# The first block of a decoder trunk: how a conditioning vector, x and two of its rows reach the engines

## The chip, the cores and the metric

The kernel runs on one core of a Trainium2 chip. The core has five engines with a queue of instructions each: TensorE (PE: matrix products and transposes), VectorE (DVE), ScalarE (ACT), GpSimd (POOL) and SyncE (SP, which here only issues DMA transfers). The metric is the device time of one execution in microseconds (us), the median of several.

## The reference

One layer of a hybrid decoder over x (2048 tokens by 1024 channels), float32. A condition vector c (1024) gives 6 x 1024 numbers that shift, scale and gate the two sub-layers:

```python
c_act = jax.nn.silu(c)
mod = (c_act @ w_ada[l] + b_ada[l])[:, None, :]
sh1, sc1, g1, sh2, sc2, g2 = jnp.split(mod, 6, axis=-1)
h = rms_norm(x) * (1.0 + sc1) + sh1
x = x + g1 * token_mixer(h, w_in[l], ...)
h = rms_norm(x) * (1.0 + sc2) + sh2
x = x + g2 * conv_ffn(h, w_up[l], ...)
return rms_norm(x) * final_gain
```

Only the start matters here: the first 512 tokens of `x`, the first two parts of `mod` (sh1 and sc1), `h` for those tokens, and the first products `h @ w_in`.

## The kernel before, in words

Channels lie on the 128 partitions, so x is 8 tiles (k = 0 to 7) of 128 channels, and tokens are taken in blocks of 512. `mod` is kept as 48 columns of 128 numbers: columns 0 to 7 are sh1, 8 to 15 are sc1. A column m needs the 128 x 1024 tile `wada[m]` (512 KB). `ada(m)`, called as `cond(m)` in the first block, is one DVE instruction (line 199): it multiplies that tile by `c_act`, in which the whole of silu(c) stands on every partition, and adds up along the row into `mod[:, m]`; a second, tiny DVE row reads the sum out. `c_act` comes from `craw`, a DMA that copies c to all 128 partitions (line 178).

Products are made at nearly float32 precision from rounded parts: a weight tile is cast on ACT to a high part (`hf`, `hq`, `hv0`, `hv1`, line 408, later `hhfh`, `hhqh`, `hvgh`, line 242), and DVE subtracts to get the low part (`lf`, `lq`, `lv`, line 412). Likewise h for channel tile k is made in three steps: `scaled` (DVE, line 365, x times scale times `bc`, the spread 1/rms), `high` (ACT, line 369, adds the shift and rounds) and `low` (DVE, line 372). Each k then feeds 18 products of TensorE ("the products of k", lines 453 and 459): two with `hf`, two with `hq`, eight with `hv`, one with `lf`, one with `lq`, four with `lv`. The first product of k needs `high`, the second needs `low`.

`startup()` writes out this first block by hand, and the order in which it calls things is the order of the DVE, ACT and SP queues there; TensorE's order is also the written one everywhere. Behind the first block the tile framework orders DVE, ACT and SP by priorities. Before the loop over k come the squares of x (`sumsq`: ACT squares, line 358, DVE adds, line 359), four products that sum them over channels (`ssn`), Newton steps for 1/sqrt on DVE, and `bcn`, which spreads the result (copied to `bc` by ACT, line 442). The loop over k is driven by the table `plan`.

What follows the first block starts with the next head's products `pshfh` (line 254). The four accumulators of TensorE are all in use by the first block, so the first of these products must wait until ACT has read the accumulator of `hf` twice (`sfh` and `snh`, two sigmoids, lines 742 and 743); ACT also makes that head's weight parts. Weight tiles are loaded into two buffers (`NRAW = 2`), so the load of `rv0` (third weight tile) waits until `lf` has been made from the first. `masks` (224 KB) and `alraw` (64 KB) are two small inputs that are needed later; both take a buffer of the pool `te`, and so do all tiles made by `tmp()`. Low parts are also written back to DRAM for reuse (`keep`, tiles `kepti0l`, `kepti1l` and so on).

Of the kernel before, what the change touches and what calls it, by code (L numbers as in the profile page):

```python
# [18 lines left out]
P = 128  # L19
# [85 lines left out]
def trunk(ctx, tc, xT, vecs, cvec, cst, rope, msk, wada, win, walow, wgla, wout, wup, wdown, out):  # L105
# [33 lines left out]
    def small(name, n=8):  # L139
        return pc.tile([P, n], F32, tag="sm", name=name, bufs=8)  # L140

    V, S, G, T = nc.vector, nc.scalar, nc.gpsimd, nc.tensor

    vec = pc.tile([P, NV], F32, tag="vec", name="vec")
    nc.sync.dma_start(vec[:], vecs)
    c_all = pc.tile([P, NC_], F32, tag="cst", name="c_all")
    m_all = p1.tile([P, NM], U32, tag="msk", name="m_all")
    ident = c_all[:, C_ID:C_ID + P]
    causal = c_all[:, C_CAUS:C_CAUS + P]
    ones = c_all[:, C_ONE:C_ONE + 1]  # L150
    nc.sync.dma_start(c_all[:], cst)

    def newton(x, y, n):

# [19 lines left out]


    c_act = pa.tile([P, D], F32, tag="a4k", name="c_act")
    craw = pa.tile([P, D], F32, tag="a4k", name="craw")
    nc.sync.dma_start(craw[:], cvec.to_broadcast([P, D]))
    S.activation(c_act[:], craw[:], AF.Sigmoid)
    V.tensor_tensor(c_act[:], c_act[:], craw[:], op=ALU.mult)  # L180
    mod = pc.tile([P, 48], F32, tag="mod", name="mod")

    bada1 = vec[:, V_BADA:V_BADA + 48]
# [180 lines left out]
    def scaled(t, bc, k):  # L364
        V.scalar_tensor_tensor(t, t, SC1[:, k:k + 1], bc, op0=ALU.mult, op1=ALU.mult)

    def high(t, k, name):
        h[k] = ph.tile([P, 2, TB], F32R, tag="h", name=f"ha{name}{k}", bufs=8)
        S.activation(h[k][:, 0, :], t, AF.Identity, bias=SH1[:, k:k + 1])

    def low(t, k):
        V.scalar_tensor_tensor(h[k][:, 1, :], t, SH1[:, k:k + 1], h[k][:, 0, :], op0=ALU.add, op1=ALU.subtract)
# [5 lines left out]
    def x_tile(name, k):  # L378

        if k % 2 == 0:  # L380
            pair[0] = px.tile([P, SB], F32, tag="xy", name=name, bufs=4)
        return pair[0][:, (k % 2) * TB:(k % 2 + 1) * TB]
# [6 lines left out]
    def startup():  # L389


        x, W, pending = [], {}, []
        for k in range(KD):
            x.append(x_tile(f"x0_{k}", k))
            nc.sync.dma_start(x[k], xT[0, :, k, :])
        raws = {}

        def weight(name, i, extra=False):
            raw = pw.tile([P, 1024], F32, tag="wraw", name="r" + name, bufs=NRAW)
            nc.sync.dma_start(raw[:], win[i])  # L400
            if extra:
                t = [pa.tile([P, 1024], F32R, tag="a4k", name=n + name) for n in "hl"]
            else:
                t = [pw.tile([P, 1024], F32R, tag="w" + n, name=n[0] + name) for n in ("hi", "lo")]
            W[name] = [*t, raw, i]

        def cast(name):
            S.copy(W[name][0][:], W[name][2][:])

        def low_part(name):  # L410
            hi, lo, raw, i = W[name]
            V.tensor_tensor(lo[:], raw[:], hi[:], op=ALU.subtract)

        def cond(m):
            ada(m, raws.pop(m))

        def load(*ms):
            for m in ms:
                raws[m] = ada_load(m, True)
        load(8, 0)  # L420
        weight("f", 1)
        load(9)
        weight("q", 0)
        load(1, 2)
        acc = new_acc("n1_0")
        for k in range(KD):
            sumsq(acc, x[k], k, "n1_0_")
        cond(8)
        ps = late_ps("ssn1_0")
        for c in range(NCH):  # L430
            T.matmul(ps[:, c:c + 1], acc[:, c * P:(c + 1) * P], ones, start=True, stop=True)
        ms, r = small("msn1_0", NCH), small("rsn1_0", NCH)
        V.tensor_scalar(ms[:], ps[:, 0:NCH], 1.0 / D, EPS, op0=ALU.mult, op1=ALU.add)
        newton(ms, r, NCH)
        cast("f")
        bc = bc1[0] = new_bc1(0)
        ps = late_ps("bcn1_0")
        for c in range(NCH):
            T.transpose(ps[:, c * P:(c + 1) * P], r[:, c:c + 1].to_broadcast([P, P]), ident)
        cond(0)  # L440
        cond(9)
        S.copy(bc[:], ps[:])
        cast("q")
        pf, pq = acc_ps("pshfh0_0"), acc_ps("pshqh0_0")
        pv = [acc_ps(f"psvgh0_0_{j}") for j in range(NCH // 2)]

        def put(kind, k, w):

            two = (0, 1) if w == 0 else (0,)
            if kind in "fq":  # L450
                sl = slice(k * P, (k + 1) * P)
                for p in two:
                    T.matmul((pf if kind == "f" else pq)[:], W[kind][w][:, sl], h[k][:, p, :],
                             start=k == 0 and w == 0 and p == 0, stop=k == KD - 1 and w == 1, skip_group_check=True)
            else:
                sl = slice((k % 4) * 256, (k % 4 + 1) * 256)
                for c in range(NCH):
                    for p in two:
                        T.matmul(pv[c // 2][:, (c % 2) * 256:(c % 2) * 256 + 256], h[k][:, p, c * P:(c + 1) * P],
                                 W[f"v{k // 4}"][w][:, sl], start=k == 0 and w == 0 and p == 0 and c % 2 == 0,  # L460
                                 stop=k == KD - 1 and w == 1 and c % 2 == 1, skip_group_check=True)

        def flush():
            for q in list(pending):
                if (q[0] if q[0] in "fq" else f"v{q[1] // 4}") in parts[q[2]]:
                    pending.remove(q)
                    put(*q)

        plan = [((10,), (), (1,), "f"), ((3, 11), (), (2,), "q"), ((4,), (10,), (3,), "v0"),
                ((12, 5), (11,), (4,), None), ((13, 6), (12,), (5,), "v1"), ((14, 7), (13,), (6,), None),  # L470
                ((15,), (14,), (7,), None), ((), (15,), (), None)]
        parts = {"f", "q"}, set()
        for k, (ld, first, then, wl) in enumerate(plan):
            if k == 0:
                weight("v0", 2)
            if k == 3:
                weight("v1", 3, True)
            load(*ld)
            for m in first:
                cond(m)  # L480
            scaled(x[k], bc[:], k)
            high(x[k], k, "0_")
            if k in (1, 4):
                name = "v0" if k == 1 else "v1"
                cast(name)
                parts[0].add(name)
            for m in then:
                cond(m)
            low(x[k], k)
            if wl:  # L490
                low_part(wl)
                parts[1].add(wl)
            pending += [(kind, k, w) for w in (0, 1) for kind in "fqv"]
            flush()
        assert not pending
        ready["hfh0_0"], ready["hqh0_0"], ready["vgh0_0"] = pf, pq, pv
        return W

# [1162 lines left out]
```

## Time and profile before

| what | us |
|---|---|
| median of 3 runs (lowest, highest) | 2534.34 (2533.82, 2537.03) |
| the profiled execution | 2533.74 |
| its span, from first to last instruction | 2532.0 |
| TensorE busy (97% of the span) | 2454.5 |
| VectorE busy (79%) | 1988.6 |
| ScalarE busy (46%) | 1153.5 |
| first product of line 453 | 22.82 |
| first product behind the first block (line 254) | 58.88 |

The profile is one execution; its time is 1.7 us over its span. Start times below are counted from the first instruction. A busy share of 97% for TensorE says that nearly all time behind the first block is TensorE's own work, which the change leaves in the same order.

### The profile page before, as it was taken

The numbers are of one execution on the slowest core, as the hardware profiler recorded it, in microseconds if no ns is written. First come the engines' busy times: TensorE is split into PE (matmuls) and PEld (weight loads), VectorE is DVE, ScalarE is ACT, GpSimd is POOL, SyncE is SP. The second block draws the span as 40 slices with busy tenths as digits, with TensorE's granted clock in tenths as the row PEclk, the third lists the DMA queues.
The fourth block names the chain that finished last, engine by engine and source line by source line (L and its number), as shares of the span: only waits on it lengthen the run. The fifth ranks groups of instructions, "written<-read, shape, count | busy, mean of one in ns | idle before, by whom it ended". The sixth has DMA issues, their size and how long they took to land.

```text
span 2532.0 us, 35188 instructions
## 1 busy us (share of the span) xinstructions
PE 2454.5 (97%) x12173; PEld 2064.3 (82%) x12173; DVE 1988.6 (79%) x3642; ACT 1153.5 (46%) x1960; POOL 150.0 (6%) x278
## 2 busy tenths in 40 slices
PE   5999999999999999999899999999989999999998
PEld 4888878888888888788788888888878888888887
DVE  8987887877688685877798888887688777778666
ACT  3333424434443334434455455555445555555453
POOL 1000000000000000000110000000001010010000
PEclk9999999999999999999999999999999999999999
DMA  8854459865688647884654544587665544447763
GB/s 309 296 163 134 169 181 320 289 225 169 218 284 310 223 159 242 308 303 161 215 187 149 168 154 138 168 283 242 209 219 170 160 138 150 152 136 256 218 191 133
DMA packets 232498, 525.11 MB, mean 207 GB/s; under 512 B 24928, under 2 KB 28032, under 8 KB 232320
## 3 DMA queue, kind: packets, MB, share of 16 engines
q1 hardware_dynamic: 229120, 512.38, 61.2%
q0 software_dynamic: 3200, 10.49, 1.2%
q8 instruction: 96, 1.57, 0.2%
q14 instruction: 82, 0.67, 0.1%
HBM read 397.46 MB, written 125.30 MB: 206 GB/s over the span
## 4 chain that ended last, share of the span: by engine, by line
PE 46%; DMA 2%; DVE 1%; issue 1%; ACT 0%; DVEq 0%; POOL 0%; SPq 0%; ACTq 0%; POOLq 0%
PE X L254 6%; PE X L255 6%; PE X L256 6%; PE Z L254 3%; PE Z L255 3%; PE Z L256 3%; PE dX L254 3%; PE dX L256 3%; PE dX L255 3%; PE dY L254 2%; PE dY L256 2%; PE dY L255 2%; PE Y L254 2%; PE Y L255 2%; PE Y L256 2%
## 5 line engine op out<-in xcount | busy, mean ns | idle before, releaser
L254 PE MATMUL X<-B,A 128*128 128x512 f32 x572 | 224.5, 392 | 1.8 <-ACT u L1355 1.8
L256 PE MATMUL X<-B,A 128*128 128x512 f32 x572 | 223.8, 391 | 0.0
L255 PE MATMUL X<-B,A 128*128 128x512 f32 x572 | 223.8, 391 | 0.0
L1055 DVE TENSOR_TENSOR dA<-rd,dA 128x512 fp32r<-128x512 f32 x154 | 105.9, 689 | 85.9 <-ACT dA L1054 85.7
L1054 ACT CAST dA<-rd 128x512 fp32r<-128x512 f32 x154 | 95.6, 621 | 134.3 <-PE dY L256 44.7
L1055 DVE TENSOR_TENSOR A<-s,A 128x512 fp32r<-128x512 f32 x176 | 120.5, 685 | 39.0 <-ACT A L1054 38.6
L1054 ACT CAST A<-s 128x512 fp32r<-128x512 f32 x176 | 108.7, 618 | 69.1 <-PE Z L256 44.9
L254 PE MATMUL dX<-dB,dA 128*128 128x512 f32 x352 | 136.9, 389 | 0.0
L255 PE MATMUL dX<-dB,dA 128*128 128x512 f32 x352 | 136.9, 389 | 0.0
L256 PE MATMUL dX<-dB,dA 128*128 128x512 f32 x352 | 136.9, 389 | 0.0
L254 PEld LDWEIGHTS X<-B,A 128*128 128x128 f32 x572 | 108.2, 189 | 25.4 <-ACT u L1355 3.1
L256 PEld LDWEIGHTS X<-B,A 128*128 128x128 f32 x572 | 108.1, 189 | 22.8
L255 PEld LDWEIGHTS X<-B,A 128*128 128x128 f32 x572 | 108.1, 189 | 22.3
L254 PE MATMUL Z<-B,A 128*128 128x512 f32 x308 | 119.9, 389 | 0.0
L255 PE MATMUL Z<-B,A 128*128 128x512 f32 x308 | 119.8, 389 | 0.0
L256 PE MATMUL Z<-B,A 128*128 128x512 f32 x308 | 119.8, 389 | 0.0
L1055 DVE TENSOR_TENSOR dB<-rb,dB 128x512 fp32r<-128x512 f32 x154 | 105.4, 685 | 11.5 <-ACT dB L1054 11.5
L1055 DVE TENSOR_TENSOR A<-r,A 128x512 fp32r<-128x512 f32 x130 | 89.3, 687 | 29.5 <-ACT A L1054 29.3
L662 PEld LDWEIGHTS lvh<-qbh,kh 128*128 128x128 f32 x768 | 100.1, 191 | 14.4 <-issue 7.3
L1054 ACT CAST A<-r 128x512 fp32r<-128x512 f32 x130 | 80.8, 622 | 63.7 <-PE Z L256 59.2
L662 PE MATMUL lvh<-qbh,kh 128*128 128x128 f32 x768 | 102.1, 275 | 5.5 <-DVE kh L672 5.2
L254 PE MATMUL psqkvgr<-hqkvgr,ha 128*128 128x512 f32 x256 | 106.1, 414 | 1.1 <-DVE orsg L160 1.0
(479 smaller groups left out, 7000.2 us busy)
## 6 DMA issues: line engine op xcount, KB each, us to landing
gs<-yv SPq DMA_DIRECT2D x154, 256.0 KB, 3.0
rb<-gs SPq DMA_DIRECT2D x154, 256.0 KB, 4.1
r<-wup SPq DMA_DIRECT2D x140, 256.0 KB, 3.4
s<-sumsu SPq DMA_DIRECT2D x136, 256.0 KB, 3.2
wada<-wada SPq DMA_DIRECT2D x48, 512.0 KB, 6.6
rd<-sumsd SPq DMA_DIRECT2D x88, 256.0 KB, 3.8
rd<-wdown SPq DMA_DIRECT2D x66, 256.0 KB, 4.0
x<-xT SPq DMA_DIRECT2D x64, 256.0 KB, 5.9
```

Source lines behind the costliest of these rows:

```text
L254: T.matmul(ps, lhs[0], rhs[0], start=first, stop=False, skip_group_check=more)
L255: T.matmul(ps, lhs[0], rhs[1], start=False, stop=False, skip_group_check=more)
L256: T.matmul(ps, lhs[1], rhs[0], start=False, stop=last, skip_group_check=more)
L662: T.matmul(ps[:, c * P:(c + 1) * P].rearrange("p (h n s) -> p h n s", h=2, s=s), kq[:, c * P:(c + 1) * P], rhs, start=True, stop=True)
L1054: S.copy(hi, src)
L1055: V.tensor_tensor(lo, src, hi, op=ALU.subtract)
```

## The change

1. The condition vector is loaded as 8 rows of 128 numbers (`c8`), silu is taken on those, and TensorE spreads them over the partitions: eight products with a column of the identity matrix, repeated 128 times (`cc0`, `cc1`), copied to `c_act` half by DVE and half by ACT. A transposed copy `ccol` is made as well.
2. x comes in four transfers of 512 KB in place of eight of 256 KB, with the first tiles of `wada` between them; `masks` and `alraw` are issued later.
3. Columns 15 and 7 of `mod` are made by TensorE: `row_spread` transposes the tile `wada[m]` in eight pieces (`wt15`, `wt7`) that ACT copies out, `row_sum` makes one row of 128 sums with eight products (`wm15`, `wm7`), which ACT copies (`wr15`, `wr7`), and `row_end` turns the row into a column with one product (`we15`, `we7`), which ACT adds the bias to. `row_spread` stands behind k = 2 and 4, `row_sum` behind 3 and 5, `row_end` behind 4 and 6.
4. The other columns are made by DVE at other places; `cond(8)` and `cond(0)` come ahead of the Newton steps. A table `steps` sets the order for each k (s = scaled, c = cond, h = high, l = low).

```diff
@@ -141,14 +141,16 @@
 
     V, S, G, T = nc.vector, nc.scalar, nc.gpsimd, nc.tensor
 
+    c_all = pc.tile([P, NC_], F32, tag="cst", name="c_all")
+    nc.sync.dma_start(c_all[:], cst)
+    c8, c8s = (tmp(n)[:, 0:P] for n in ("c8", "c8s"))
+    nc.sync.dma_start(c8[0:KD, :], cvec.rearrange("o (k p) -> (o k) p", p=P))
     vec = pc.tile([P, NV], F32, tag="vec", name="vec")
     nc.sync.dma_start(vec[:], vecs)
-    c_all = pc.tile([P, NC_], F32, tag="cst", name="c_all")
     m_all = p1.tile([P, NM], U32, tag="msk", name="m_all")
     ident = c_all[:, C_ID:C_ID + P]
     causal = c_all[:, C_CAUS:C_CAUS + P]
     ones = c_all[:, C_ONE:C_ONE + 1]
-    nc.sync.dma_start(c_all[:], cst)
 
     def newton(x, y, n):
 
@@ -174,10 +176,9 @@
 
 
     c_act = pa.tile([P, D], F32, tag="a4k", name="c_act")
-    craw = pa.tile([P, D], F32, tag="a4k", name="craw")
-    nc.sync.dma_start(craw[:], cvec.to_broadcast([P, D]))
-    S.activation(c_act[:], craw[:], AF.Sigmoid)
-    V.tensor_tensor(c_act[:], c_act[:], craw[:], op=ALU.mult)
+    ccol = small("ccol", KD)
+    S.activation(c8s[0:KD, :], c8[0:KD, :], AF.Sigmoid)
+    V.tensor_tensor(c8s[0:KD, :], c8s[0:KD, :], c8[0:KD, :], op=ALU.mult)
     mod = pc.tile([P, 48], F32, tag="mod", name="mod")
 
     bada1 = vec[:, V_BADA:V_BADA + 48]
@@ -389,11 +390,11 @@
     def startup():
 
 
-        x, W, pending = [], {}, []
-        for k in range(KD):
-            x.append(x_tile(f"x0_{k}", k))
-            nc.sync.dma_start(x[k], xT[0, :, k, :])
-        raws = {}
+        x, W, pending, raws = [], {}, [], {}
+
+        def x_load(i):
+            x.extend((x_tile(f"x0_{2 * i}", 0), x_tile(f"x0_{2 * i + 1}", 1)))
+            nc.sync.dma_start(pair[0][:].rearrange("p (a n) -> p a n", a=2), xT[0, :, 2 * i:2 * i + 2, :])
 
         def weight(name, i, extra=False):
             raw = pw.tile([P, 1024], F32, tag="wraw", name="r" + name, bufs=NRAW)
@@ -417,30 +418,71 @@
         def load(*ms):
             for m in ms:
                 raws[m] = ada_load(m, True)
-        load(8, 0)
+
+        def row_spread(m):
+
+            raw, halves = raws.pop(m), []
+            for j in range(2):
+                p = lev_ps(f"wt{m}_{j}")
+                for i in range(4):
+                    T.transpose(p[:, i * P:(i + 1) * P], raw[:, (4 * j + i) * P:(4 * j + i + 1) * P], ident)
+                t = tmp(f"wt{m}_{j}")
+                S.copy(t[:], p[:])
+                halves.append(t)
+            return m, halves
+
+        def row_sum(m, halves):
+            p = late_ps(f"wm{m}")
+            for i in range(KD):
+                T.matmul(p[0:1, 0:P], ccol[:, i:i + 1], halves[i // 4][:, (i % 4) * P:(i % 4 + 1) * P],
+                         start=i == 0, stop=i == KD - 1)
+            row = tmp(f"wr{m}")
+            S.copy(row[0:1, 0:P], p[0:1, 0:P])
+            return m, row
+
+        def row_end(m, row):
+            p = late_ps(f"we{m}")
+            T.matmul(p[:, 0:1], row[0:1, 0:P], ones[0:1, :], start=True, stop=True)
+            S.activation(mod[:, m:m + 1], p[:, 0:1], AF.Identity, bias=bada1[:, m:m + 1])
+
+        x_load(0)
+        load(8)
+        x_load(1)
+        load(0)
+        x_load(2)
+        x_load(3)
+        load(9)
         weight("f", 1)
-        load(9)
+        load(1)
         weight("q", 0)
-        load(1, 2)
+        load(10, 2)
+        for j in range(2):
+            p = lev_ps(f"cc{j}")
+            for i in range(4 * j, 4 * j + 4):
+                T.matmul(p[:, (i % 4) * P:(i % 4 + 1) * P], ident[0:KD, i:i + 1].to_broadcast([KD, P]), c8s[0:KD, :],
+                         start=True, stop=True)
+            (S.copy if j else V.tensor_copy)(c_act[:, j * 512:(j + 1) * 512], p[:])
+        p = late_ps("ccol")
+        T.transpose(p[:, 0:KD], c8s[0:KD, :], ident[0:KD, 0:KD])
+        S.copy(ccol[:], p[:, 0:KD])
+        cond(8)
         acc = new_acc("n1_0")
         for k in range(KD):
             sumsq(acc, x[k], k, "n1_0_")
-        cond(8)
+        cond(0)
         ps = late_ps("ssn1_0")
         for c in range(NCH):
             T.matmul(ps[:, c:c + 1], acc[:, c * P:(c + 1) * P], ones, start=True, stop=True)
         ms, r = small("msn1_0", NCH), small("rsn1_0", NCH)
         V.tensor_scalar(ms[:], ps[:, 0:NCH], 1.0 / D, EPS, op0=ALU.mult, op1=ALU.add)
         newton(ms, r, NCH)
-        cast("f")
         bc = bc1[0] = new_bc1(0)
         ps = late_ps("bcn1_0")
         for c in range(NCH):
             T.transpose(ps[:, c * P:(c + 1) * P], r[:, c:c + 1].to_broadcast([P, P]), ident)
-        cond(0)
         cond(9)
+        cast("f")
         S.copy(bc[:], ps[:])
-        cast("q")
         pf, pq = acc_ps("pshfh0_0"), acc_ps("pshqh0_0")
         pv = [acc_ps(f"psvgh0_0_{j}") for j in range(NCH // 2)]
 
@@ -466,33 +508,43 @@
                     pending.remove(q)
                     put(*q)
 
-        plan = [((10,), (), (1,), "f"), ((3, 11), (), (2,), "q"), ((4,), (10,), (3,), "v0"),
-                ((12, 5), (11,), (4,), None), ((13, 6), (12,), (5,), "v1"), ((14, 7), (13,), (6,), None),
-                ((15,), (14,), (7,), None), ((), (15,), (), None)]
-        parts = {"f", "q"}, set()
-        for k, (ld, first, then, wl) in enumerate(plan):
+        loads = [(11,), (3, 15, 12), (4, 7), (13, 5, 14), (6,), (), (), ()]
+        casts = ["q", "v0", None, "v1", None, None, None, None]
+        steps = ["s0 c1 h lf l c10", "s1 h c2 lq l", "s2 h c11 lv0 l", "s3 c3 h c12 l", "s4 c4 h lv1 l c13",
+                 "s5 c5 h c14 l", "s6 c6 h s7 l", "h l"]
+        parts = {"f"}, set()
+        rows = []
+        for k in range(KD):
             if k == 0:
                 weight("v0", 2)
-            if k == 3:
+            if k == 2:
                 weight("v1", 3, True)
-            load(*ld)
-            for m in first:
-                cond(m)
-            scaled(x[k], bc[:], k)
-            high(x[k], k, "0_")
-            if k in (1, 4):
-                name = "v0" if k == 1 else "v1"
-                cast(name)
-                parts[0].add(name)
-            for m in then:
-                cond(m)
-            low(x[k], k)
-            if wl:
-                low_part(wl)
-                parts[1].add(wl)
+            load(*loads[k])
+            for st in steps[k].split():
+                kind, what = st[0], st[1:]
+                if kind == "s":
+                    scaled(x[int(what)], bc[:], int(what))
+                elif kind == "c":
+                    cond(int(what))
+                elif kind == "h":
+                    high(x[k], k, "0_")
+                    if casts[k]:
+                        cast(casts[k])
+                        parts[0].add(casts[k])
+                elif what:
+                    low_part(what)
+                    parts[1].add(what)
+                else:
+                    low(x[k], k)
             pending += [(kind, k, w) for w in (0, 1) for kind in "fqv"]
+            if k in (2, 4):
+                rows.append(row_spread({2: 15, 4: 7}[k]))
             flush()
-        assert not pending
+            if k in (3, 5):
+                rows.append(row_sum(*rows.pop()))
+            if k in (4, 6):
+                row_end(*rows.pop(0))
+        assert not pending and not rows
         ready["hfh0_0"], ready["hqh0_0"], ready["vgh0_0"] = pf, pq, pv
         return W
 
```

ScalarE's queue around k = 3 to 6, before (`ha0_k` is the high part of h for tile k, `hhfh` and `hhqh` belong to the next head):

```order
L369 ACTIVATE ha0_3_529<-x0_2_348,mod_104 128x512
L369 ACTIVATE ha0_4_557<-x0_4_351,mod_104 128x512
L408 CAST hv1_521<-rv1_519 128x1024
L242 CAST hhfh0_1_722<-rhfh0_1_724 128x1024
L369 ACTIVATE ha0_5_587<-x0_4_351,mod_104 128x512
L369 ACTIVATE ha0_6_613<-x0_6_354,mod_104 128x512
```

The same place in the changed kernel:

```order
L370 ACTIVATE ha0_3_564<-x0_2_351,mod_106 128x512
L409 CAST hv1_504<-rv1_502 128x1024
L440 COPY wr15_596<-wm15_587 1x128
L370 ACTIVATE ha0_4_602<-x0_4_355,mod_106 128x512
L430 COPY wt7_0_612<-wt7_0_607 128x512
L430 COPY wt7_1_619<-wt7_1_614 128x512
L446 ACTIVATE mod_106<-we15_639,vec_89 128x1
L243 CAST hhfh0_1_789<-rhfh0_1_791 128x1024
L370 ACTIVATE ha0_5_644<-x0_4_355,mod_106 128x512
L440 COPY wr7_675<-wm7_666 1x128
L370 ACTIVATE ha0_6_679<-x0_6_357,mod_106 128x512
```

Between the `high` steps stand copies that read what TensorE has just made: `wr15` ahead of `ha0_4`, the bias step of `we15` ahead of `ha0_5`, `wr7` ahead of `ha0_6`.

ScalarE's queue at the end of the first block, before:

```order
L369 ACTIVATE ha0_7_637<-x0_6_354,mod_104 128x512
L242 CAST hhqh0_1_763<-rhqh0_1_765 128x1024
L742 ACTIVATE sfh0_0_685<-pshfh0_0_429 128x512
L743 ACTIVATE snh0_0_686<-pshfh0_0_429 128x512
L748 ACTIVATE sqh0_0_691<-pshqh0_0_430 128x512
```

And in the changed kernel (`alow` is cast from the late input `alraw`, `hvgh` is a weight part of the next head, which stood eight rows further back):

```order
L829 CAST alow_123<-alraw_734 128x8x16
L446 ACTIVATE mod_106<-we7_701,vec_89 128x1
L370 ACTIVATE ha0_7_704<-x0_6_357,mod_106 128x512
L243 CAST hhqh0_1_830<-rhqh0_1_832 128x1024
L243 CAST hvgh0_1_0_905<-rvgh0_1_0_907 128x1024
L794 ACT_TABLE_LOAD
L794 ACTIVATE sfh0_0_752<-pshfh0_0_443 128x512
L795 ACTIVATE snh0_0_753<-pshfh0_0_443 128x512
```

A cast, a load of ScalarE's function table and, further up, the cast of `alow` now stand ahead of the two sigmoids.

TensorE's queue from the last products of k = 3 to the first of k = 4, before:

```order
L453 MATMUL pshqh0_0_430<-ha0_3_529,lq_370 128x512
L459 MATMUL psvgh0_0_0_431<-lv0_436,ha0_3_529 128x256 x2
L459 MATMUL psvgh0_0_1_432<-lv0_436,ha0_3_529 128x256 x2
L453 MATMUL pshfh0_0_429<-ha0_4_557,hf_363 128x512 x2
L453 MATMUL pshqh0_0_430<-ha0_4_557,hq_369 128x512 x2
```

In the changed kernel:

```order
L495 MATMUL pshqh0_0_444<-ha0_3_564,lq_370 128x512
L501 MATMUL psvgh0_0_0_445<-lv0_450,ha0_3_564 128x256 x2
L501 MATMUL psvgh0_0_1_446<-lv0_450,ha0_3_564 128x256 x2
L437 MATMUL wm15_587<-wt15_0_521,ccol_103 1x128 x4
L437 MATMUL wm15_587<-wt15_1_528,ccol_103 1x128 x4
L428 MATMUL wt7_0_607<-c_all_84,wada7_508 128x128 x4
L428 MATMUL wt7_1_614<-c_all_84,wada7_508 128x128 x4
L495 MATMUL pshfh0_0_443<-ha0_4_602,hf_363 128x512 x2
```

The sums `wm15` stand behind all products of k = 3, and the transposes `wt7` between them and k = 4. From the next head on TensorE's rows are the same in both kernels.

## Rows read from the trace of the kernel before

**Rows 1.** Stretches: us; busy us and count of each engine; TensorE clock, DMA share, GB/s.

```profile
45.00:50.00 5.00, 3.33 (x15) 2.54 (x14) 4.93 (x10) 0.84 (x2) 0.00 (x0) 0.83 0.94 373
...
140.00:150.00 10.00, 10.00 (x68) 8.95 (x66) 6.52 (x18) 4.92 (x10) 0.90 (x2) 1.00 0.85 276
```

**Rows 2.** TensorE in order of time: start, us, operation, [idle before <- releaser].

```profile
29.75 2.08 PE L459 MATMUL psvgh<-hv,ha 128*128 128x256 f32 x8 [3.74 <-ACT hv L408]
...
42.13 0.39 PE L453 MATMUL pshfh<-ha,hf 128*128 128x512 f32 x1
...
47.91 0.50 PE L453 MATMUL pshfh<-ha,hf 128*128 128x512 f32 x1 [0.62 <-DVE ha L372]
...
52.13 0.62 PE L453 MATMUL pshfh<-ha,hf 128*128 128x512 f32 x2
...
54.93 0.39 PE L453 MATMUL pshfh<-ha,hf 128*128 128x512 f32 x1
55.56 0.50 PE L453 MATMUL pshfh<-ha,hf 128*128 128x512 f32 x1 [0.23 <-DVE ha L372]
...
58.88 0.50 PE L254 MATMUL pshfh<-ha,hhfh 128*128 128x512 f32 x1 [0.48 <-ACT snh L743]
...
68.52 0.60 PE L639 MATMUL dth<-c_all,xh 128*128 128x128 f32 x4
...
73.66 1.07 PE L662 MATMUL lvh<-qbh,kh 128*128 128x128 f32 x8
74.48 0.37 PE L254 MATMUL psvgh<-hvgh,ha 128*128 128x256 f32 x1
...
177.62 0.50 PE L254 MATMUL psvgh<-hvgh,ha 128*128 128x512 f32 x1 [3.66 <-DVE sqh L749]
```

**Rows 3.** VectorE in order of time, from the sums to the last low part.

```profile
9.38 5.47 DVE L359 TENSOR_TENSOR san<-san,sqn 128x512 f32<-128x512 f32 x7 [0.77 <-ACT sqn L358]
...
16.80 0.16 DVE L433 TENSOR_SCALAR msn<-ssn 128x4 f32<-128x4 f32 x1 [0.76 <-PE ssn L431]
...
21.26 0.74 DVE L365 SCALAR_TENSOR_TENSOR x<-x,mod,bc 128x512 f32<-128x512 f32 x1
21.93 1.27 DVE L199 CUSTOM_DVE_ANT_0 wada<-wada,c_act,vec 128x1024 f32<-128x1024 f32 x1
...
23.13 0.74 DVE L372 SCALAR_TENSOR_TENSOR ha<-x,mod,ha 128x512 fp32r<-128x512 f32 x1
23.80 1.22 DVE L412 TENSOR_TENSOR lf<-rf,hf 128x1024 fp32r<-128x1024 f32 x1
...
54.76 0.74 DVE L372 SCALAR_TENSOR_TENSOR ha<-x,mod,ha 128x512 fp32r<-128x512 f32 x1
```

**Rows 4.** ScalarE in order of time, first block.

```profile
3.17 0.20 ACT L168 ACTIVATE lbe<-lbe 128x4 f32<-128x4 f32 x1 [1.15 <-DVE lbe L167]
3.39 1.28 ACT L179 ACT_TABLE_LOAD   x1
...
20.14 0.59 ACT L442 COPY bc<-bcn 128x512 f32<-128x512 f32 x1 [2.50 <-PE bcn L439]
...
28.65 1.04 ACT L408 CAST hv<-rv 128x1024 fp32r<-128x1024 f32 x1 [2.21 <-DMA rv<-win]
...
46.02 0.72 ACT L369 ACTIVATE ha<-x,mod 128x512 fp32r<-128x512 f32 x1 [2.38 <-DVE x L365]
...
56.09 1.05 ACT L242 CAST hhqh<-rhqh 128x1024 fp32r<-128x1024 f32 x1 [1.63 <-PE pshfh L453]
57.74 0.60 ACT L742 ACTIVATE sfh<-pshfh 128x512 f32<-128x512 f32 x1 [0.60 <-PE pshfh L453]
58.24 0.59 ACT L743 ACTIVATE snh<-pshfh 128x512 f32<-128x512 f32 x1
```

**Rows 5.** DMA issues of the first 60 us: count, KB, us from issue to landing.

```profile
kepti5l<-lhfh SPq DMA_DIRECT2D x1, 512.0 KB, 3.1
...
alraw<-walow SPq DMA_DIRECT2D x1, 64.0 KB, 8.4
```

## The prediction

> **What bounds the kernel now.** I read the table of stretches first. Late in the first block VectorE works 4.93 of 5 us while TensorE works 3.33 and its clock is partly lowered (0.83 over the stretch) [rows 1]; so there the chain of VectorE sets the pace. Then I followed the engines in order of time. Behind 58.88, where the next head's products begin, TensorE keeps its own order in both kernels, and a shift of that row shifts the end. The one long wait for VectorE further on, 3.66 us at 177.62, comes after a stretch (140 to 150) in which VectorE has 3.5 us to spare, so VectorE's earlier backlog is gone by then and the wait will come again, only later [rows 1, 2]. So the question is when the row at 58.88 starts. It waits for the second sigmoid, which ends at 58.83, which waits for the products of k = 7, which wait for the last low part at 54.76 to 55.50 [rows 2 to 4].
>
> **The front.** Spreading c takes eight products. Before has none so early; the nearest are the `lvh` products, four in 74.48 - 73.66 = 0.82 us, 0.205 each [rows 2]. The engine is cold here, so I take twice that, 3.3 us for eight. c8 is there at about 4 (VectorE's first row, which lets ScalarE's row at 3.17 go, waits for the same transfers [rows 4]); 4 + 3.3, a copy out of at most 0.59 and column 8 at 1.20 (21.93 to 23.13) give 9.1, while the adds now start at 9.38 [rows 3, 4]. They are seven in 5.47 us, held by ScalarE's squares as much as by x, so x in four transfers gains nothing here, and neither loses as long as the last pair lands by some 12.5. Column 0 fills the wait for `ssn` (which ends at 16.80) that column 8 fills now [rows 3]. One column fewer stands behind the Newton steps: the first `scaled` can start when `bc` is copied, 20.14 + 0.59 = 20.73, in place of 21.26: -0.5 us [rows 3, 4]. Bounds: 0 and +2, the latter if the spread is late by its whole 2 x 0.82.
>
> **What VectorE gains.** Columns 15 and 7 leave it (2.4 us) and column 0 is out of the chain. From 20.73 to `scaled` of k = 4 it has four `scaled` and four `low` at 0.67, six columns at 1.20 and three low weight parts at 1.22: 5.4 + 7.2 + 3.7 = 16.2, so x of k = 4 is ready at 36.9 + 0.75 = 37.7 [rows 3].
>
> **What TensorE and ScalarE get.** The load of `rv0` waits for `lf`. `lf` now stands ahead of `low` of k = 0, so it is 0.67 + 0.5 earlier, and the cast of `hv0` (28.65) and the first `hv` products (29.75) move to 28.6 [rows 2 to 4]. From there to the first product of k = 4 TensorE takes 42.13 - 29.75 = 12.38 us without a pause [rows 2]. It now also does the transposes `wt15` (two rows like the one of 0.60 for four, with run-out: 1.0 together) and the eight sums `wm15` at 0.205, 1.64 [rows 2]. That is 28.6 + 12.4 + 1.0 + 1.7 = 43.7. ScalarE's queue has `wr15`, which waits for these sums, ahead of `high` of k = 4. A small ScalarE row is 0.20 [rows 4]; with the notice 0.25. So `high` of k = 4 starts at 43.95, 6.2 us after its input is ready, and VectorE's gain is spent waiting.
>
> From then on the two engines hand over to each other, since each `high` stands behind a copy that needs the end of TensorE's work on the k before. One round: `high` 0.72, `low` 0.75 and two notices of 0.06 (46.02 + 0.72 = 46.74; 47.91 is the second product of k = 5), and 2.57 from the second product to the end of the 18: at the full clock k = 6 takes 54.93 - 52.13 = 2.80, less 0.23 for the first (0.62 for two, 0.39 for one) [rows 2 to 4]. That is 4.16.
> - k = 4: plus `we15` (0.2 and its run-out 0.1), the bias step 0.25, and the cast `hhfh`, which now stands ahead of `high`: 0.95 (a cast row is 1.05 and overlaps the next by 0.1) [rows 4]. 5.66; `high` of k = 5 at 49.6.
> - k = 5: plus `wm7` 1.64 + 0.15 and `wr7` 0.25: 6.2; k = 6 at 55.8.
> - k = 6: plus `we7` and the bias step: 4.7; k = 7 at 60.5.
> - k = 7: 1.59 to the second product; `hhqh` is free 0.53 later (55.56 to 56.09) and takes 1.0; behind it now stand `hvgh` 1.0, a table load 1.28 (before, the sigmoids found their table loaded) and the sigmoids 0.50 + 0.64 (57.74, 58.24, 58.88) [rows 2, 4]. 6.55; the next head starts at 67.05.
>
> That is 67.05 - 58.88 = +8.2 us. The waits of 1 to 2 us in each round are like those ahead of 47.91, behind which k = 5 ran at the lower clock: 52.13 - 47.91 = 4.22 in place of 2.57 [rows 1, 2]. I take one such round, +1.65; bounds none and four. Then 2533.74 + 9.85 = 2543.6 for an execution like the profiled one; the median of before lies 0.6 above that one, so **2544.2**.
>
> ScalarE's table load in the trace starts 0.02 us after the row ahead of it ends (3.37 to 3.39) and takes 1.28, which is what the sum has [rows 4]. The Trainium skill, "ScalarE: Activation LUTs", "What ACT_TABLE_LOAD costs", gives 1.28 for the load, as the row has it, but 2.66 for a switch with a drain. By that the time would be 1.4 higher; the row shows no drain ahead of it, and what follows it there waits for a transfer.
>
> Hidden: `masks` now come some 35 us later, but its readers on VectorE are the steps of the next head's `lvh`, the first of which is at 73.66; if they were later than that, TensorE would wait [rows 2]. The halves of `c_act` on ScalarE and the copies `wt15`, `wt7` (0.59 each) run while ScalarE has nothing else, or while TensorE works on the k before.
>
> **Rivals.**
> - *VectorE still sets the pace, faster.* If TensorE had `wm15` done by 37.7, the chain would be VectorE's: 37.7, then five columns, two weight parts and seven steps of 0.67 (6.0 + 2.4 + 4.7) end the last `low` at 50.8 rather than 55.50, and from there 0.06 + 0.53 + 1.0 + 1.0 + 1.28 + 1.14 = 5.0 rather than 3.38: start at 55.8, -3.1, 2531.2. For it speaks that VectorE was the bound [rows 1]; against it that TensorE would have to do in 9 us what the rows give 15 for. Chance 0.05.
> - *Within 0.2%* (5.1 us, about what a measurement tells from no change). If TensorE's first products ran at the full clock (three k at 2.80 and 1.7 of k = 0 are 10.1 in place of 12.4, -2.3), no round fell to the lower one (-1.65) and the four small copies cost 0.1 each less notice (-0.8): +5.1 or less. 0.08.
> - *`alraw` late.* `high` of k = 7 also stands behind the cast of `alow`, and `alraw` is issued behind `kepti5l`, which waits for `lhfh`. VectorE ends `low` of k = 5 at 51.1, then two `scaled`, column 6 and `lhfh` end at 54.9. A write like `kepti5l` lands in 3.1, with `masks` and `alraw` behind it some 0.8 more: 58.8, ahead of 60.5, no cost. In the crowded queue of before `alraw` took 8.4 [rows 5]: 63.3, +2.8 or 2547. 0.15.
> - *The clock falls in every round.* Three rounds more at 1.65: +4.95, 2549.2. For it: each round has the pattern of 45 to 48 [rows 1, 2]; against: k = 6 and 7 of before also had short waits and ran at full. 0.12. The Trainium skill, "TensorE: Matmul & The Clock Gate", "A second HAM failure mode: psum-queue depth-cycling", tells of a kernel whose short pauses between groups of matmuls make the clock swing between its two levels; by that rule this would be the outcome, and the trace has it in one round of eight so far.
>
> **How the numbers follow.** The forecast itself (0.60) has its own range of 2541.5 to 2547. The low end of the whole range, 2539, leaves out the faster case and most of the one within 0.2%; the high end 2549.5 takes in both later cases. Slower by over 0.2%: 0.60 + 0.15 + 0.12 = 0.87; within 0.08; faster 0.05.
>
> **What would show it.** In the new profile `high` of k = 4 waits for TensorE's `wm15` by way of `wr15`, starting near 44 while its `scaled` was done near 38; the four `high` rows then stand 5.7, 6.2 and 4.7 apart; a table load stands just ahead of `sfh`; the first `pshfh` of the next head starts near 67 to 69, TensorE's order and later waits unchanged. If ScalarE's `high` of k = 4 follows its `scaled` at once, the step of TensorE's lag is wrong and the first rival holds. If the shift at the next head is there but not at the end, the step that nothing further on takes it back is wrong.

## The result, and the profile after

The changed kernel took 2546.23 us (median of 7 runs, 2539.47 to 2550.71); the kernel before took 2533.82 on the same chip (7 runs, 2529.89 to 2538.14). The ratio is 1.0048 with an interval of 1.0035 to 1.0060: about 12 us slower, between 9 and 15. The forecast was 2544.2 with a range of 2539.0 to 2549.5.

The profiled execution of the changed kernel was its fastest, 2539.47 us with a span of 2537.6. Busy times hardly moved: TensorE 2459.8 us (before 2454.5), VectorE 1984.8 (1988.6), ScalarE 1155.9 (1153.5). What moved is the waiting in the first block. TensorE in order of time, in the form of [rows 2]:

```profile
29.69 2.07 PE L501 MATMUL psvgh<-hv,ha 128*128 128x256 f32 x8 [1.75 <-ACT hv L409]
...
42.20 1.91 PE L437 MATMUL wm<-wt,ccol 128*1 128x128 f32 x16
44.04 1.09 PE L428 MATMUL wt<-c_all,wada 128*128 128x128 f32 x8
45.07 0.50 PE L495 MATMUL pshfh<-ha,hf 128*128 128x512 f32 x1
...
50.93 0.51 PE L495 MATMUL pshfh<-ha,hf 128*128 128x512 f32 x1 [1.91 <-ACT ha L370]
...
57.37 0.49 PE L495 MATMUL pshfh<-ha,hf 128*128 128x512 f32 x1 [0.97 <-ACT ha L370]
...
62.40 0.49 PE L495 MATMUL pshfh<-ha,hf 128*128 128x512 f32 x1 [1.10 <-ACT ha L370]
...
68.25 0.49 PE L255 MATMUL pshfh<-ha,hhfh 128*128 128x512 f32 x1 [0.68 <-ACT snh L795]
...
111.40 0.66 PE L739 MATMUL kTh<-c_all,kh 128*128 128x128 f32 x4 [1.24 <-DVE kh L724]
...
189.10 0.50 PE L255 MATMUL psvgh<-hvgh,ha 128*128 128x512 f32 x1 [3.65 <-DVE sqh L801]
```

The products of `hv` begin at 29.69 (before 29.75 [rows 2]). TensorE then works through to the end of the row sums `wm` and the transposes `wt`; k = 4 starts at 45.07 where before has 42.13 for the first product of that k. From there each k begins with a wait for ScalarE's `ha` (1.91, 0.97 and 1.10 for k = 5 to 7). The next head starts at 68.25, 9.37 behind the 58.88 of before. ScalarE's rows say why:

```profile
8.79 0.64 ACT L356 ACTIVATE san<-x 128x512 f32<-128x512 f32 x1
...
12.33 1.15 ACT L359 ACTIVATE sqn<-x 128x512 f32<-128x512 f32 x2 [0.90 <-DMA x<-xT]
...
44.14 0.25 ACT L440 COPY wr<-wm 1x128 f32<-1x128 f32 x1 [6.20 <-PE wm L437]
44.30 0.72 ACT L370 ACTIVATE ha<-x,mod 128x512 fp32r<-128x512 f32 x1
...
49.07 0.26 ACT L446 ACTIVATE mod<-we,vec 128x1 f32<-128x1 f32 x1 [3.10 <-PE we L445]
...
50.16 0.72 ACT L370 ACTIVATE ha<-x,mod 128x512 fp32r<-128x512 f32 x1
56.44 0.25 ACT L440 COPY wr<-wm 1x128 f32<-1x128 f32 x1 [5.56 <-PE wm L437]
56.60 0.72 ACT L370 ACTIVATE ha<-x,mod 128x512 fp32r<-128x512 f32 x1
59.86 0.30 ACT L829 CAST alow<-alraw 128x128 fp32r<-128x128 f32 x1 [2.55 <-DMA alraw<-walow]
61.33 0.26 ACT L446 ACTIVATE mod<-we,vec 128x1 f32<-128x1 f32 x1 [1.17 <-PE we L445]
61.63 0.72 ACT L370 ACTIVATE ha<-x,mod 128x512 fp32r<-128x512 f32 x1
63.81 1.05 ACT L243 CAST hhqh<-rhqh 128x1024 fp32r<-128x1024 f32 x1 [1.46 <-PE pshfh L495]
64.76 1.04 ACT L243 CAST hvgh<-rvgh 128x1024 fp32r<-128x1024 f32 x1
65.82 1.28 ACT L794 ACT_TABLE_LOAD   x1
67.11 0.60 ACT L794 ACTIVATE sfh<-pshfh 128x512 f32<-128x512 f32 x1
```

`wr` waits 6.20 us, until `wm` is done, and only as it leaves the engine does the `high` step of k = 4 start, at 44.30. The same pairs follow: the bias step of `we` and `hhfh` ahead of k = 5 (50.16), `wr` ahead of k = 6 (56.60), the bias step ahead of k = 7 (61.63), which `high` of k = 7 itself reads (it is column 7). At the end stand `hhqh`, `hvgh` and a table load of 1.28 ahead of the first sigmoid at 67.11. VectorE, which set the pace before, now waits:

```profile
38.00 0.74 DVE L366 SCALAR_TENSOR_TENSOR x<-x,mod,bc 128x512 f32<-128x512 f32 x1
38.66 1.28 DVE L200 CUSTOM_DVE_ANT_0 wada<-wada,c_act,vec 128x1024 f32<-128x1024 f32 x1
39.87 0.08 DVE L200 DVE_READ_ACCUMULATOR2_ANT mod<- 128x1 f32 x1
...
45.06 0.75 DVE L373 SCALAR_TENSOR_TENSOR ha<-x,mod,ha 128x512 fp32r<-128x512 f32 x1 [3.79 <-ACT ha L370]
...
57.35 0.75 DVE L373 SCALAR_TENSOR_TENSOR ha<-x,mod,ha 128x512 fp32r<-128x512 f32 x1 [2.01 <-ACT ha L370]
```

Its `scaled` of k = 4 starts at 38.00 and is done at 38.7. `high` of k = 4 also reads column 4, which VectorE makes right behind it and reads out by 39.95; so `high` is ready at 39.95 and stands 4.35 us behind `wr`. The `low` of the same k comes at 45.06 after 3.79 us of idling, and that of k = 6 after another 2.01. In stretches (columns as in [rows 1]) the change of roles reads in one line, 40 to 45: TensorE 5.00 busy, VectorE 1.23; before had 4.60 and 4.96 there.

```profile
40.00:45.00 5.00, 5.00 (x40) 4.05 (x38) 1.23 (x1) 0.86 (x3) 0.00 (x0) 1.00 0.97 359
...
50.00:55.00 5.00, 3.79 (x23) 3.01 (x24) 4.30 (x8) 0.88 (x2) 0.00 (x0) 1.00 0.09 35
55.00:60.00 5.00, 3.74 (x26) 2.75 (x25) 1.09 (x2) 1.01 (x3) 0.61 (x4) 1.00 0.69 216
...
70.00:110.00 40.00, 39.88 (x249) 34.41 (x247) 39.91 (x77) 10.28 (x17) 1.04 (x2) 1.00 0.81 277
...
490.00:500.00 10.00, 10.00 (x54) 8.58 (x53) 6.56 (x12) 5.21 (x9) 0.00 (x0) 1.00 0.93 331
1040.00:1050.00 10.00, 10.00 (x68) 9.07 (x67) 7.77 (x17) 4.87 (x10) 1.04 (x2) 1.00 0.97 342
1050.00:1060.00 10.00, 5.59 (x21) 4.33 (x20) 8.06 (x24) 2.95 (x11) 0.00 (x0) 0.84 0.85 280
1250.00:1260.00 10.00, 8.67 (x41) 6.95 (x40) 8.59 (x15) 5.29 (x11) 1.06 (x2) 1.00 0.87 275
```

The stretch from 70 to 110 shows what follows: VectorE works 39.91 of 40 us (39.47 before). It has nothing to spare there, so it cannot make up what it starts late. It starts the next head's first step, `fh`, at 69.13 in place of 58.94, 10.19 later, as the framework has put `lvgh` ahead of that step. The wait at 111.40 is 1.24 us for VectorE, and the wait that [rows 2] has at 177.62 comes at 189.10 and is as long as before (3.65). So 9.37 at the next head has become 11.5 at 189. That VectorE's full queue is the reason is read from these rows; no run tests it.

That these two profiled executions end only 5.6 us apart is in the main the clock's doing. Later on the one of before was granted the lower of TensorE's two levels (1.2 of 2.4 GHz) for longer:

```profile
490.00:500.00 10.00, 8.04 (x39) 6.80 (x37) 7.01 (x20) 2.94 (x5) 0.00 (x0) 0.83 0.85 273
1040.00:1050.00 10.00, 5.17 (x20) 3.96 (x19) 8.56 (x26) 2.95 (x11) 0.00 (x0) 0.75 0.83 280
1050.00:1060.00 10.00, 10.00 (x53) 8.46 (x52) 8.25 (x14) 2.61 (x4) 0.00 (x0) 0.91 0.87 303
1250.00:1260.00 10.00, 8.96 (x29) 6.98 (x29) 7.04 (x16) 4.51 (x10) 1.06 (x2) 0.67 0.71 208
```

By what is missing to 1.00 in these four stretches, before lost 1.7 + 2.5 + 0.9 + 3.3 = 8.4 us of granted clock and the changed kernel 1.6. Row by row, TensorE's shift between the two traces is 10.5 us at 490 and 9.2 at 500, 9.9 at 1040 and 8.8 at 1060, 8.8 at 1100 and 6.5 at 1260: 4.7 of the 6.0 us by which 11.5 has shrunk at the last rows. These spells of the lower level differ from execution to execution (the 7 runs have mean clocks of 0.990 to 0.993, and spans of 2548.9 to 2537.6 in that order); the medians, 12.4 apart, are close to the 11.5 that the program itself is late at 189.

### The profile page after: what moved, and what is told of

It is laid out like the page before. It is cut to its first block, busy times and chain, and to the rows that moved or that the text cites. A ratio compares the mean times of both kernels' runs of the same rounds, so it can differ in the third digit from the quotient of the medians.

```text
span 2537.6 us, 35347 instructions
## 1 busy us (share of the span) xinstructions
PE 2459.8 (97%) x12242; PEld 2067.8 (81%) x12242; DVE 1984.8 (78%) x3639; ACT 1155.9 (46%) x1971; POOL 146.4 (6%) x278
## 4 chain that ended last, share of the span: by engine, by line
PE 46%; DMA 2%; DVE 2%; issue 1%; ACT 0%; DVEq 0%; SPq 0%; POOL 0%; ACTq 0%; POOLq 0%
PE X L255 6%; PE X L257 6%; PE X L256 6%; PE Z L257 3%; PE Z L255 3%; PE Z L256 3%; PE dX L255 3%; PE dX L256 3%; PE dX L257 3%; PE dY L257 2%; PE dY L256 2%; PE dY L255 2%; PE Y L257 2%; PE Y L255 2%; PE Y L256 1%
```

## The experiments

Each is compared with the kernel before on the same chip, in five rounds; the first row is the result above. The rows come from more than one chip, so whole times of different rows are compared by their ratios. "Next head" is the start of its first product: 58.88 before, 68.25 after the change.

| run | next head, us | ratio to before (95%) |
|---|---|---|
| the change | 68.25 | 1.0048 (1.0035 to 1.0060) |
| e1, columns on VectorE | 67.81 | 1.0047 (1.0032 to 1.0062) |
| e5, front only | 67.08 | 1.0049 (1.0030 to 1.0067) |
| e7, as e1, late `alraw` | 60.69 | 1.0004 (0.9994 to 1.0014) |
| e8, as e5, late `alraw` | 60.78 | 1.0010 (1.0001 to 1.0018) |
| e10, as e7, early table | 59.84 | 1.0001 (0.9992 to 1.0009) |
| e3, the change, early table | 68.18 | 1.0041 (1.0028 to 1.0055) |
| e12, copies behind `high` | 63.16 | 1.0024 (1.0014 to 1.0034) |
| e2, as e12, column 7 earlier | 60.85 | 1.0029 (1.0017 to 1.0041) |
| e6, as e2, early table | 60.34 | 1.0014 (1.0003 to 1.0026) |
| e11, as e6, early `rv0` | 60.64 | 1.0025 (1.0013 to 1.0037) |

**e1 and e5: the row work taken out, and the front alone.** e1 gives columns 15 and 7 back to VectorE and loads their tiles in the order of use:

```diff
-        "s5 c5 h c14 l", "s6 c6 h s7 l", "h l"]
+        "s5 c5 h c14 l", "s6 c6 h c15 s7 l", "c7 h l"]
-            if k in (2, 4):
-                rows.append(row_spread({2: 15, 4: 7}[k]))
...
```

> The changed kernel with columns 15 and 7 back on VectorE; the spreading of c, the four transfers of x and the other places of the columns stay. Theory (the hand-over between TensorE and ScalarE that the row work puts into the first block is the loss): no copy stands between the high steps, so VectorE sets the pace again. From its scaled of k = 4 at 38.0 (profile of the changed kernel) it has eight steps of 0.67, seven columns of 1.20 and two weight parts of 1.14, which ends the last low part at 54.0; then 0.06 + 0.53, hhqh 1.0, the table load 1.28 and the sigmoids 1.14: the next head starts at 58.1, where before has 58.88 and the changed kernel 68.25. The whole is within 3 us of before. Rival (the front, that is the spread of c, the transfers of x and the order of the other columns, carries part of the loss): the next head starts later than 60, and the whole is 3 to 6 us over before.

e5 is the kernel before with the first two parts of the change (c by TensorE, x in four transfers) and no other.

> The kernel before with the spreading of c by TensorE and x in four transfers alone; columns and their places, and ScalarE's queue in the loop over k, are those of before. Theory (the front is worth nothing, since the cast of hv0 is set by the load of rv0): first products of hv within 0.5 us of before (29.75), next head at 58.9 within 1 us, the whole within 3 us of before. Rival (the front is late): the changed kernel has its first product 0.8 later and the second 1.9 later than before; if that carries through the block, the next head is 1 to 2 us late and so is the whole.

Both came out as slow as the whole change, which no theory had said. ScalarE in e1, in order of time:

```profile
13.19 0.63 ACT L359 ACTIVATE sqn<-x 128x512 f32<-128x512 f32 x1 [0.17 <-DVE san L360]
21.36 0.30 ACT L823 CAST alow<-alraw 128x128 fp32r<-128x128 f32 x1 [7.54 <-DMA alraw<-walow]
21.56 1.14 ACT L359 ACTIVATE sqn<-x 128x512 f32<-128x512 f32 x2
```

The cast of `alow` stands between the sixth and the seventh square of x, and waits 7.54 us for the transfer of `alraw` (in e5 6.50, ahead of the last square). The sums of x, and all behind them, wait with it. The framework had put the cast there. In the changed kernel it falls behind `high` of k = 6; that the row tiles hold the pool `te`, from which `alraw` takes its buffer, is argued from the code. So neither run says anything of the row work; the next two take the cast out of the way.

**e7 and e8: the same two, with `alraw` called for behind the first head.**

```diff
-    gla_weights()
...
             if (b, i) == (0, 1):
+                gla_weights()
```

> The first experiment (columns 15 and 7 on VectorE) once more, with alraw and the cast of alow called for behind the first head, so that the cast doesn't stand among the squares of x. Theory (the hand-over is the loss; the 7.5 us of the first experiment were the cast's wait for alraw): sums end near 16 as in the changed kernel, VectorE goes through to the last low part at 54.0, next head at 58.1 (before 58.88), the whole within 3 us of before. Rival (VectorE is late for another reason in this order of the columns, or TensorE falls behind): next head later than 60.

> The front alone (c spread by TensorE, x in four transfers) on the kernel before, with alraw called for behind the first head. Theory (the front is neutral but for the function table: the exponential now stands behind the first sigmoid, so the sigmoids at the end of the block find the wrong table): VectorE's chain as in before or 0.8 us behind it, plus 1.28 less what is hidden: next head at 59.5 to 61, the whole 0.5 to 2 over before. Rival (the front is late by itself, whatever the cast of alow): next head later than 62.

Without the row work the loss is gone: e7 is not told apart from before. (The place of `alow` is not what makes the change slow: its cast ends there at 60.2, ahead of the bias step at 61.33, which waits for TensorE.) Its next head is 2.6 later than worked out; two reasons stand in ScalarE's rows:

```profile
45.74 1.04 ACT L243 CAST hhfh<-rhfh 128x1024 fp32r<-128x1024 f32 x1 [4.88 <-DMA rhfh<-win]
...
55.09 0.72 ACT L370 ACTIVATE ha<-x,mod 128x512 fp32r<-128x512 f32 x1 [4.27 <-DVE mod L200]
```

`hhfh`, ahead of `high` of k = 5, waits 4.88 us for its tile, so VectorE idles 0.96 there; the last column stands ahead of `high` of k = 7 (55.09) and VectorE idles 0.79 behind it; smaller gaps make the rest.

e8 has the front by itself. ScalarE, then TensorE:

```profile
8.70 0.59 ACT L436 COPY c_act<-cc 128x512 f32<-128x512 f32 x1 [3.92 <-PE cc L434]
9.19 0.63 ACT L355 ACTIVATE san<-x 128x512 f32<-128x512 f32 x1
```

```profile
15.89 1.86 PE L443 MATMUL ssn<-c_all,san 128*128 128x1 f32 x8 [7.22 <-DVE san L359]
...
44.11 0.50 PE L465 MATMUL pshfh<-ha,hf 128*128 128x512 f32 x1 [0.60 <-DVE ha L372]
...
60.78 0.50 PE L254 MATMUL pshfh<-ha,hhfh 128*128 128x512 f32 x1 [1.20 <-ACT snh L755]
```

Here, too, a copy of TensorE's results stands ahead of work that is ready: ScalarE's half of `c_act` waits 3.92 us for the spread, and the first square of x follows it at 9.19 (8.10 in the trace of before). The sums start at 15.89, 1.00 behind before, and the 1.0 to 1.2 stays to k = 4 (44.11 against 42.91); the wait of 1.20 ahead of the next head, 0.48 before, is the table load. Together 1.9 at the next head, inside what was expected; in the whole 1.0010, or 2.5 us, where 0.5 to 2 was expected.

**e12 and e2: the place of the copies.** In e12 TensorE's order is that of the change, and ScalarE's copies of row results stand behind the next `high`, all but the bias step of column 7. In e2, moreover, TensorE makes the sums of column 7 behind k = 4 rather than 5 and its row end behind k = 5 rather than 6, so that the bias step, which `high` of k = 7 needs, waits for the products of k = 5 and not of k = 6. The transposes `wt7` stay where they were: in the change, too, they stand ahead of the products of k = 4 (44.04), as `wt15` stands ahead of those of k = 2.

```diff
-            S.copy(row[0:1, 0:P], p[0:1, 0:P])
+            todo.append(lambda: S.copy(row[0:1, 0:P], p[0:1, 0:P]))
...
                     high(x[k], k, "0_")
+                    while todo:
+                        todo.pop(0)()
```

> All row work stays on TensorE (16 transposes, 16 sums, two row ends), but each ScalarE copy of its results now stands behind the next high instead of ahead of it, and the work for column 7 begins one k earlier. Theory (the place of the copies in ScalarE's queue is the loss, not TensorE's own time for the row work): high of k = 4 starts at 38.8, as soon as its input is ready, VectorE does not wait 3.8 us there, and TensorE works through: k = 3 with wm15 and wt7 to 45, then four k at 2.8 and the small sums, so k = 7 starts near 56 and the next head near 61; 7 us less than the changed kernel there, and 5 to 8 us less in the whole, that is 4 to 7 over before. Rival (TensorE's added 6 us are what is lost, wherever the copies stand): the next head starts at 67 to 68 as in the changed kernel, and the whole is 10 to 12 over before.

> The changed kernel with nothing moved on TensorE: only the ScalarE copies of the row work stand behind the next high, where that can be. The last one, the bias step of column 7, must stay ahead of high of k = 7, since that reads it, so one hand-over is left. Theory (each hand-over costs by itself): as with the late copies up to high of k = 6, TensorE without a pause there; then high of k = 7 waits for we7 behind the products of k = 6 and TensorE waits about 1.1 plus 0.3 for it, as it does in the changed kernel ahead of k = 7; the next head starts 1.4 later than with the late copies (60.85), near 62.3, and the whole is 1 to 2 us above them. Rival (the earlier start of column 7 was what helped, not the place of the copies): the next head starts later than 65.

ScalarE in e2:

```profile
39.70 0.72 ACT L370 ACTIVATE ha<-x,mod 128x512 fp32r<-128x512 f32 x1 [1.11 <-DVE mod L200]
44.61 0.25 ACT L440 COPY wr<-wm 1x128 f32<-1x128 f32 x1 [4.18 <-PE wm L437]
```

`high` of k = 4 starts at 39.70, 4.6 earlier than in the change (38.8 was expected; the rest is its wait for column 4), and `wr` waits behind it at nobody's cost. TensorE in e2:

```profile
45.35 0.71 PE L495 MATMUL pshfh<-ha,hf 128*128 128x512 f32 x2
...
56.69 0.62 PE L495 MATMUL pshfh<-ha,hf 128*128 128x512 f32 x2
...
60.85 0.50 PE L255 MATMUL pshfh<-ha,hhfh 128*128 128x512 f32 x1 [1.20 <-ACT snh L799]
```

It makes all of the row work and has not one wait between k = 4 and the end of k = 7; the next head comes 7.4 earlier. In e12 one hand-over is left, and it shows just there:

```profile
58.33 0.51 PE L495 MATMUL pshfh<-ha,hf 128*128 128x512 f32 x1 [1.10 <-ACT ha L370]
```

TensorE waits 1.10 and then 0.28 in k = 7, and the next head, at 63.16, is 2.3 behind e2's (1.4 expected). So the place of the copies is worth 5.1 us at the next head, of which 1.0 is `hvgh`, which the framework now puts behind the sigmoids (from `high` of k = 7 to the next head 63.16 - 57.56 = 5.60 in place of 6.62); the earlier column 7 gives another 2.3. What is left is 1.97 against before, and 0.16 against e7 (60.69), which has the same front and makes these columns on VectorE; so with the copies out of the way TensorE's added work costs about what VectorE gains by it. In the whole e12 and e2 aren't told apart.

**e3, e6 and e10: the function table.** One unused sigmoid of four numbers behind the exponential of the start:

```diff
     S.activation(e[:], e[:], AF.Exp)
+    S.activation(t[:], e[:], AF.Sigmoid)
```

> The changed kernel with one more tiny sigmoid (4 numbers, unused) on ScalarE right behind the exponential of the start, so that the function table of the sigmoids is loaded near 5 us, where ScalarE has 3.4 us free, and not at 65.8. Theory (the table load is a term of the tail): the next head starts 1.2 earlier than in the changed kernel, at 67.0, if TensorE has its full clock in k = 7, and 0.3 earlier if the clock is lowered there, since the first sigmoid then waits for the product at 66.76; the whole is 0.3 to 1.3 less than the changed kernel. Rival (the load is hidden behind products of k = 7 that end later anyway): no difference at the next head.

> The late copies of the second experiment together with the early load of the sigmoid table of the third. Theory (with the copies behind the high steps the tail is hhqh, table load and two sigmoids, and TensorE ends k = 7 ahead of it): the wait of 1.20 ahead of the next head goes; it starts at 59.6 where the late copies alone have 60.85, before has 58.88 and the changed kernel 68.25. The whole is 1.2 less than the late copies alone. Rival (the first sigmoid waits for the last product of hf anyway): no difference to 60.85.

> The run with columns 15 and 7 on VectorE and alraw late, with the sigmoid table loaded near 5 us as well. Theory: the next head starts 1.2 us earlier than in that run, near 56.9, that is 2 us ahead of before, and the whole is 1 to 3 us less than before, which a comparison can just miss. Rival (TensorE's last products of k = 7 end later than the sigmoids could start): next head as in that run.

In e3 the first sigmoid then waits 0.80 for the product of k = 7, which ran at the lower clock there; from `high` of k = 7 to the next head it takes 68.18 - 62.15 = 6.03 in place of 68.25 - 61.63 = 6.62. In e6: TensorE waits 0.48 ahead of the next head, as in before, in place of e2's 1.20. In e10 it waits 0.48 too, in place of 1.21 in e7; the next head comes at 59.84 and not at the 56.9 that was expected, since e7 had already missed 58.1. The table load is a term of the tail, and gives 0.5 to 0.9 of its 1.28 back; the rest was beside TensorE's last products.

**e11: TensorE's chain begun earlier**, with `rv0` among the first transfers in a buffer of its own, and `hv0` cast behind `hq`.

> Late copies and early table, and the third weight tile rv0 loaded among the first transfers into a buffer of its own (one that a high part uses later), so that hv0 is cast behind hq and TensorE need not wait for it from 27.9 to 29.7. Theory (with the late copies TensorE sets the pace from 29.7 on): its chain starts some 2 us earlier, and the next head starts near 58.5, where late copies and early table have 60.3 and before has 58.88; the whole is within 2 us of before. Rival (VectorE's low parts set the pace as soon as TensorE is ahead): next head at 59.5 or later.

The rival held. TensorE begins the products of `hv` without the wait at 27.9, and meets VectorE instead, where the framework has now put the next head's `lhfh` ahead of column 14 and `low` of k = 5:

```profile
46.70 1.23 DVE L250 TENSOR_TENSOR lhfh<-rhfh,hhfh 128x1024 fp32r<-128x1024 f32 x1 [0.60 <-issue]
47.84 1.28 DVE L202 CUSTOM_DVE_ANT_0 wada<-wada,c_act,vec 128x1024 f32<-128x1024 f32 x1
```

That `low` starts at 49.05, and TensorE waits 0.32 for it in k = 5 and 0.81 for the one of k = 6. With the row work on TensorE and its copies out of the way, the two engines are about even. No run beat the kernel before.

## Why the prediction was right

*The hand-over.* This was the core, and it held: VectorE's gain is spent waiting for `high`, which stands behind a copy of TensorE's results. Predicted and measured starts of `high`: k = 4 43.95 and 44.30, k = 5 49.6 and 50.16, k = 6 55.8 and 56.60, k = 7 60.5 and 61.63. That it is mostly the queue's order, e12 and e2 show: of the 9.37 at the next head the place of the copies alone gives back 4.1 (5.1 less `hvgh`), and 7.4 are gone once the sums of column 7 come earlier as well. In the whole these runs give back about half (1.0048, and 1.0024 and 1.0029). One reading in the sum was off: it took `high` of k = 4 as ready with its x, at 37.7, and 6.2 us as its wait. The step also reads column 4, which comes one column later, so it waited 4.35 us (39.95 to 44.30), and VectorE 3.79.

*Two errors that cancelled.* The step "`lf` now stands ahead of `low` of k = 0 ... and the first `hv` products (29.75) move to 28.6" failed: they start at 29.69, since the front is late. But TensorE needs 14.35 from there to the end of the sums at 44.04, where 15.1 was allowed, mostly since its products reach the full rate earlier: the eight of `hv` in k = 1 take 1.10 at 33.27, and 1.51 at 33.76 before. That the two leave only 0.35 (44.30 for 43.95) is luck.

*The front* was given -0.5 and is +1.0 to +1.2 (e8). The sum had a price for the copy of `c_act`, but not its place ahead of the squares: they start at 8.79 in the changed kernel, and wait once more, 0.90 at 12.33, for the third pair of x, which has two column tiles ahead of it. `ssn` starts at 16.13 rather than 14.89. On VectorE's side this costs nothing, as an input that is ready at 39.95 still waits for 44.30. On TensorE's side it does: it is the late start at 29.69, and so 1.1 of that 44.30.

*The tail* was right: 6.55 predicted from `high` of k = 7 to the next head, 6.62 measured, table load and `hvgh` where they were said to be. The load starts at 65.82, 0.02 behind the cast, and takes 1.28. The Trainium skill, "ScalarE: Activation LUTs", "What ACT_TABLE_LOAD costs", adds a drain to each switch; none shows here either.

*The clock.* One more lowered round at 1.65 was the wrong term. Each kernel has one: k = 5 before [rows 1], k = 7 after (the eight `hv` products at 64.42 take 1.91 in place of 1.10), where ScalarE's tail covered it. In its place stand 1.2 us of a later start and longer rounds (68.25 against 67.05), and so the next head came 9.37 late where 9.85 was allowed; that these two are so close is luck too. The rival that the clock falls in every round did not come: k = 5 and 6 had waits of 1.91 and 0.97 ahead of them, and the granted clock is 1.00 in the stretches 50 to 55 and 55 to 60. (Of the two rounds that the prediction set against it, k = 6 of before had no wait ahead of it: 52.13 [rows 2].) The Trainium skill, "TensorE: Matmul & The Clock Gate", "A second HAM failure mode: psum-queue depth-cycling", tells of a kernel whose short pauses between groups of matmuls make the clock swing between its levels; these rounds do not show that.

*"A shift of that row shifts the end"* left out that VectorE has no slack from 70 to 110: 2.1 us came on top by 189. With the 9.37 that makes 11.5; the 0.9 that is left to the 12.4 between the medians is well inside their interval of 9 to 15.

*The rivals.* `alraw` was late but not late enough: the cast of `alow` ended at 60.2, ahead of the bias step at 61.33, as worked out. Not foreseen was that the same cast, early, would have cost 6.5 to 7.5 (e5, e1); what saved the change from it, its own use of the pool, is argued and not tested.

*Open.* e2, e12 and e11 are 6 to 7 us slower in the whole (by their ratios), though their next heads are only 2.0, 4.3 and 1.8 late; e6 has 3.5 for 1.5, e7 1.0 for 1.8. In e2's profile VectorE lets TensorE wait 0.51, 0.49 and 0.85 between 423 and 434, where before has no wait; row by row its TensorE is 2.2 behind at 420 and 4.8 at 450. Why there, no run tells, and so about half of the loss in the whole has no cause shown further than that e7, without the row work, does not have it.

## What to carry to other kernels

ScalarE's rows here ran in the order in which they were queued: a small copy of another engine's result, put ahead of a step that the chain needs, made that step wait for the other engine though its own input was ready (`high` of k = 4 at 44.30, and at 39.70 with the copy behind it). Before moving work to the engine with idle time, look at where its results come back and put them behind the next urgent step, a round early if need be. And when an experiment takes something out, look in its trace at what the framework has put in the freed place before reading its time.

## What the runs showed of the hardware

The eight row sums of one column (16 rows of `wm`) took 1.84 us from 42.20 to 44.04, 0.23 each, where the sum took 0.205 from a product of another shape. The spreading of c took 3.78 us for its eight products (16 rows), 0.5 more than the 3.3 of the sum. And two executions of one kernel can differ by over 11 us here (2539.47 and 2550.71) with mean granted clocks of 0.993 and 0.990 (by an estimate from these, 0.003 of 2540, some 7.6 us of full clock), so that a shift of a few us is read safely in the trace at the place where it arises, and in the whole only over many runs.
